# A hybrid attention and state-space block on one core: a recorded program with a list scheduler of its own, weight rings in 512-column blocks, and a tenth 7-product step in four gate pairs

## The chip, the core and the metric

The kernel runs on one NeuronCore of a Trainium2 chip; the other seven are idle. The metric is the device time of one execution in microseconds. Everything is float32 at the interface. PE is the matrix engine, DVE the vector engine, ACT the scalar engine, POOL the GpSimd engine (here it mostly starts transfers), SP the engine that starts most transfers.

## The reference, cut to what matters

One layer, 256 tokens, model width 4096:

```
h = rms_norm(x, pre_gain);  proj = h @ w_in          # 4096 x 24704
q, k, v, gate_a, qi, ki, wi, z, xs, bm, cm, dt, merge_logits = split(proj)
y_a = dsa_attention(rope(q), rope(k), v, rope(qi), rope(ki), wi) * silu(gate_a)   # top-64 keys by an indexer
y_b = ssd_mixer(xs, z, bm, cm, dt, ...)                                           # Mamba-2, chunked
g = sigmoid(merge_logits)                             # two gates of 4096 columns
out = (g[0] * (y_a @ w_branch_attn) + g[1] * (y_b @ w_branch_ssd)) @ w_out
x = x + rms_norm(out, post_gain)
```

Nearly all the work is in the products of 256 rows with the weights: 24,704 columns of w_in, then two branch projections (2048 to 4096) and w_out (4096 to 4096).

## The kernel before

Weights are streamed from HBM once, as float32. TensorE multiplies them in its rounding type fp32r: each operand is split into a rounded high part and a low part, and a product is three matmuls, low x high, high x low, high x high (`product`, line 598). A weight tile `raw` is split by ACT (the high part `wh`, line 548) and DVE (`wl` = raw - wh, line 552; line 550 where a sign is turned).

Big projections go in pairs of 512-column blocks (`pair_gemm`). The activations stand as 16 slots of 256 rows of the contraction (two k-tiles) by 256 tokens (two halves); one step of a pair takes one slot with a 2 x 2 block of weights (two k-tiles by two column blocks, each 128 x 512). Three kinds of steps:

- R: eight products, 24 matmuls. The weight blocks are split as they are, two at a time.
- D: also eight products, with one difference of the activations as an operand.
- S: seven products by Winograd's scheme, 21 matmuls. It needs sums and differences of the weights: POOL adds one block onto another by an accumulating transfer (line 672), DVE makes t2 (line 677) and then t3 and t4 together (line 678), and seven blocks instead of four are split. It also needs sums of the activations, kept ready in `ext` tiles for those slots that are S.

The tuples at the top of the program name the S slots of each stage: SX, SA, SS for the projections of h, SG for the gate pairs 3 to 6 (nine of 16 slots), SY for the branches, SM for the output. `SG_ORDER` is the order of the slots there.

Around the pairs runs side work: rotary, top-k, attention, the state-space scan, and the forms of the next stage's activations. It is written as generators; `step(pace)` advances the first of them after each step of a pair. Its matmuls (transposes, logits, scan products; called auxiliary below) are in plain fp32 and stand in PE's order between weight matmuls.

What sets the order: up to gate pair 1 the framework's scheduler, by priorities; from there on (`written`) the order of DVE and ACT is that in which the program is written, with the next step's first split started early (`begin`). Buffers: `raw` tiles of two blocks, eight of them (a ninth in the `late` pool from gate pair 2 on); `wh` and `wl` tiles of two blocks, five each (six late). The single block t2 takes a whole two-block tile early, and later a tile of its own, `nh` and `nl`, with one buffer.

A pair ends with evacuations: `early` (lines 602 to 604: an ACT copy and two DVE additions from PSUM), `late` and `rest`. The last pair is `ending`, followed by the last norm and the residual (`root_mean`, `final`).

Of the kernel before, what the change touches and what calls it, by code (L numbers as in the profile page):

```python
# [11 lines left out]
F32 = mybir.dt.float32  # L12
# [3 lines left out]
ALU = mybir.AluOpType  # L16
# [9 lines left out]
SBUFS = 5  # L26
RBUFS = 8
# [31 lines left out]
def fused_block(tc, x, xT, w_qi, w_misc, w_q0, w_qk, w_vg, w_x, w_z, w_gate, w_br, w_out2,  # L59
                percol, rows, tabs, tris, pgain, out):  # L60
    nc = tc.nc
# [24 lines left out]


# [39 lines left out]
    def step(n=1):  # L127
        credit[0] += n
        n = int(credit[0])
        credit[0] -= n  # L130
        while n and aux:
            try:
                next(aux[0])
            except StopIteration:
                aux.popleft()
            n -= 1
# [25 lines left out]
    rings = {"raw": (rawp, RBUFS), "wh": (whp, SBUFS), "wl": (wlp, SBUFS)}  # L162
    more_of, made = {}, {}

    def widen(pool, **counts):
        more_of.update({tag: (pool, n) for tag, n in counts.items()})
        made.update(dict.fromkeys(counts, 0))

    def ring(tag, shape, dtype):
        pool, n = rings[tag]  # L170
        if tag in more_of:
            second, m = more_of[tag]
            if made[tag] % (n + m) >= n:
                pool = second
                made[tag] += 1
                return pool.tile(shape, dtype, tag=tag, bufs=m, name=tag)
            made[tag] += 1
        return pool.tile(shape, dtype, tag=tag, name=tag)

    def raw_tile():  # L180
        return ring("raw", [P, HK, NW], F32)
# [8 lines left out]
    def gemm(chunks, nk, act, evac, prep=None, plan=None, done=None, pace=1, spill=()):  # L190
# [4 lines left out]
        plan = plan or [(h, (0, 1)) for h in range(nk // HK)]  # L195
        at = {t: [n for n, (_, tt) in enumerate(plan) if t in tt] for t in range(2)}
        raws, parts = {}, {}
        for n, (half, toks) in enumerate(plan):
            c, hf = divmod(half, KC // HK)
            if half not in raws:  # L200
                raws[half] = raw_tile()
                if prep is not None:
                    if not hf:
                        xr = prep_x(c)
                    load_half(raws[half], chunks[c], hf, c == 0)
                else:
                    load_half(raws[half], chunks[c], hf)
            if half not in parts:
                if half in spill:
                    wh, wl = (rawp.tile([P, HK, NW], F32R, tag="raw", name="wx") for _ in range(2))  # L210
                else:
                    wh = whp.tile([P, HK, NW], F32R, tag="wh", name="wh")
                    wl = wlp.tile([P, HK, NW], F32R, tag="wl", name="wl")
                parts[half] = wh, wl
                if len(parts) > SBUFS + len(spill):
                    del parts[next(iter(parts))]
                rs = raws[half]
                if prep is not None:
                    for i in range(HK):
                        split_x(half * HK + i, xr[:, hf * HK + i, :])  # L220
                        A.activation(wh[:, i, :], rs[:, i, :], AF.Copy)
                        V.tensor_sub(wl[:, i, :], rs[:, i, :], wh[:, i, :].bitcast(F32))  # L222
                else:
                    A.activation(wh, rs, AF.Copy)  # L224
                    V.tensor_sub(wl, rs, wh.bitcast(F32))  # L225
            wh, wl = parts[half]
            for i in range(HK):
                ah, al = act(half * HK + i)
                for t in toks:
                    first = n == at[t][0] and i == 0  # L230
                    last = n == at[t][-1] and i == HK - 1
# [11 lines left out]
    def gemm_misc(evac):  # L243
# [4 lines left out]
        for c in range(KT // KC):  # L248
            raw = rawp.tile([P, KC, P], F32, tag="raw", name="rawm")
            nc.sync.dma_start(raw, w_misc[c])  # L250
            wh = whp.tile([P, KC, P], F32R, tag="wh", name="whm")
            wl = wlp.tile([P, KC, P], F32R, tag="wl", name="wlm")
            A.activation(wh, raw, AF.Copy)
            V.tensor_sub(wl, raw, wh.bitcast(F32))
# [14 lines left out]
    warm = whp.tile([P, NW], F32, tag="wh", name="warm")  # L269
# [221 lines left out]
    def ext_forms(i, a, seven):  # L491
        a11, a21, a12, a22 = (a[:, k, t * P:(t + 1) * P] for k in range(2) for t in range(2))
        if i in seven:
            V.scalar_tensor_tensor(a22, a22, -1.0, a21, ALU.mult, ALU.subtract)
            V.tensor_sub(a21, a21, a11)
            V.scalar_tensor_tensor(a11, a22, -1.0, a11, ALU.mult, ALU.subtract)
            V.tensor_sub(a12, a11, a12)
            return a.rearrange("p k (t c) -> p (k t) c", t=2), 4
# [1053 lines left out]
```

## Time and profile before

| what | value |
|---|---|
| median of 3 runs | 2787.32 us (2786.72 to 2788.2) |
| span of the profiled execution | 2787.8 us |
| PE busy, PE weight loads busy | 2767.6 us (99%), 2277.0 us (82%) |
| DVE, ACT, POOL busy | 2458.2 us (88%), 1692.4 us (61%), 384.6 us (14%) |
| mean DMA rate | 235 GB/s |

Busy times are sums of instructions of one execution; TensorE's are pipelined, and their ends are modelled, so the distance between the starts of two matmuls says more than their duration (0.39 us for 128 x 512). A group's row gives its count, its busy time and mean duration, and the idle time of its engine just before it with what ended that. A row on a stretch of time gives for each engine the busy time and the number of instructions in it; an instruction on its border counts in both.

### The profile page before, as it was taken

To read this page: it belongs to the slowest core of one execution; us is meant where nothing else is said; L and a number is where in the kernel's file an instruction comes from. 1 tells how busy PE (TensorE), PEld (TensorE's weight loads), DVE (VectorE), ACT (ScalarE), POOL (GpSimd) and SP (SyncE) were. 2 spreads that over 40 slices of the span, in tenths; PEclk is the share of its full clock that TensorE was granted. 3 is DMA by queue.
4 is the path that set the end of the run, shared out by engine and by line. 5 is a ranking of instruction groups with operands and counts; after the bars stand their busy time and mean duration, and the time that the engine had idled before them with its cause. 6 is when DMAs were issued, how large, how long until landed. Compare 5 with 4: busy or idle time off the path is not lost.

```text
span 2787.8 us, 36296 instructions
## 1 busy us (share of the span) xinstructions
PE 2767.6 (99%) x12470; PEld 2277.0 (82%) x12470; DVE 2458.2 (88%) x3064; ACT 1692.4 (61%) x2217; POOL 384.6 (14%) x515
## 2 busy tenths in 40 slices
PE   9999999999999999999999999999999999999998
PEld 7877888888888888888887888888888887888886
DVE  6668989999999988887888888999999999998997
ACT  7444565565655666886677655556666545555554
POOL 0101101212112110111011111111111211220000
PEclk9999999999999999999999999999999999999999
DMA  9545787878878876666666688887888778978786
GB/s 375 194 167 171 212 241 219 261 226 234 243 222 253 227 225 217 203 197 214 197 194 200 230 257 247 247 250 238 272 270 257 251 250 253 318 229 242 240 253 209
DMA packets 206552, 655.37 MB, mean 235 GB/s; under 512 B 26272, under 2 KB 27552, under 8 KB 206368
## 3 DMA queue, kind: packets, MB, share of 16 engines
q1 hardware_dynamic: 163408, 565.74, 60.6%
q0 software_dynamic: 42240, 86.01, 14.8%
q8 instruction: 97, 1.59, 0.2%
q10 hardware_dynamic: 720, 1.31, 0.1%
q14 instruction: 87, 0.71, 0.1%
HBM read 627.79 MB, written 25.17 MB: 234 GB/s over the span
## 4 chain that ended last, share of the span: by engine, by line
PE 90%; DVE 4%; issue 3%; ACT 1%; DMA 1%; POOL 0%; POOLq 0%; SPq 0%; ACTq 0%; DVEq 0%
PE p L598 79%; PE p L233 3%; PE p L234 3%; PE p L235 3%; DVE wl L552 2%; ACT wh L548 1%; DMA raw<-w_gate_d 0%; PE p L438 0%; PE p L1033 0%; DVE raw L678 0%; PE p L898 0%; PE p L865 0%; DVE wl L225 0%; DVE raw L677 0%; PE p L1022 0%
## 5 line engine op out<-in xcount | busy, mean ns | idle before, releaser
L598 PE MATMUL p<-wh,b 128*128 128x512 f32 x4860 | 1608.0, 392 | 1.8 <-ACT wh L548 1.8
L548 ACT ACTIVATE wh<-raw 128x1024 fp32r<-128x1024 f32 (+1 forms) x1228 | 1193.5, 1016 | 514.4 <-PE p L598 235.8
L552 DVE TENSOR_TENSOR wl<-raw,wh 128x1024 fp32r<-128x1024 f32 (+1 forms) x965 | 1096.9, 1164 | 155.7 <-ACT wh L548 154.6
L598 PEld LDWEIGHTS p<-wh,b 128*128 128x128 f32 x4860 | 911.8, 188 | 193.2 <-ACT wh L548 6.4
L598 PE MATMUL p<-wl,b 128*128 128x512 f32 x2430 | 946.4, 389 | 0.7 <-DVE wl L550 0.7
L598 PE MATMUL p<-wh,ext 128*128 128x512 f32 x1958 | 692.9, 390 | 0.8 <-ACT wh L548 0.8
L598 PEld LDWEIGHTS p<-wl,b 128*128 128x128 f32 x2430 | 456.5, 188 | 95.4 <-DVE wl L550 2.4
L598 PEld LDWEIGHTS p<-wh,ext 128*128 128x128 f32 x1958 | 367.4, 188 | 78.5 <-ACT wh L548 2.7
L598 PE MATMUL p<-wl,ext 128*128 128x512 f32 x979 | 382.8, 391 | 1.0 <-DVE wl L552 0.8
L550 DVE SCALAR_TENSOR_TENSOR wl<-raw,wh 128x1024 fp32r<-128x1024 f32 x263 | 320.8, 1220 | 28.7 <-ACT wh L548 27.8
L548 ACT ACTIVATE nh<-raw 128x512 fp32r<-128x512 f32 x99 | 62.7, 633 | 319.0 <-DVE raw L677 267.7
L678 DVE TENSOR_TENSOR raw<-raw 128x1024 f32<-128x1024 f32 x200 | 244.5, 1222 | 5.4
L598 PEld LDWEIGHTS p<-wl,ext 128*128 128x128 f32 x979 | 183.7, 188 | 44.2 <-DVE wl L552 5.5
L233 PE MATMUL p<-wh,b 128*128 128x512 f32 x384 | 151.2, 396 | 1.8 <-DVE b L306 1.8
L234 PE MATMUL p<-wl,b 128*128 128x512 f32 x384 | 149.9, 390 | 0.0
L235 PE MATMUL p<-wh,b 128*128 128x512 f32 x384 | 149.6, 390 | 0.0
L225 DVE TENSOR_TENSOR wl<-raw,wh 128x1024 fp32r<-128x1024 f32 x80 | 99.4, 1243 | 52.8 <-ACT wh L224 52.6
L677 DVE TENSOR_TENSOR raw<-raw 128x512 f32<-128x512 f32 x200 | 137.7, 688 | 4.8
L224 ACT ACTIVATE wh<-raw 128x1024 fp32r<-128x1024 f32 x80 | 84.5, 1059 | 90.1 <-PE p L235 78.5
L672 POOL DMA_DIRECT2D raw<-w_gate_d x59 | 51.4, 871 | 487.8 <-DMA raw<-w_gate_d 208.5
L233 PEld LDWEIGHTS p<-wh,b 128*128 128x128 f32 x384 | 71.9, 188 | 20.2 <-issue 2.7
L234 PEld LDWEIGHTS p<-wl,b 128*128 128x128 f32 x384 | 72.1, 188 | 15.3 <-DVE wl L222 1.0
(255 smaller groups left out, 1937.7 us busy)
## 6 DMA issues: line engine op xcount, KB each, us to landing
raw<-w_gate_d SPq DMA_DIRECT2D x256, 512.0 KB, 6.0
raw<-w_vg_d SPq DMA_DIRECT2D x128, 512.0 KB, 5.3
raw<-w_x_d SPq DMA_DIRECT2D x128, 512.0 KB, 4.9
raw<-w_br_d SPq DMA_DIRECT2D x128, 512.0 KB, 6.0
raw<-w_out_d SPq DMA_DIRECT2D x128, 512.0 KB, 5.6
raw<-w_qk_d SPq DMA_DIRECT2D x96, 512.0 KB, 5.4
raw<-w_z_d SPq DMA_DIRECT2D x64, 512.0 KB, 5.2
raw<-w_qi_d SPq DMA_DIRECT2D x62, 512.0 KB, 5.9
```

The costliest lines, as they stand in the source:

```text
L224: A.activation(wh, rs, AF.Copy)
L225: V.tensor_sub(wl, rs, wh.bitcast(F32))
L233: T.matmul(ps[t], al[:, tk], wh[:, i, :], start=first, stop=False)
L234: T.matmul(ps[t], ah[:, tk], wl[:, i, :], start=False, stop=False)
L235: T.matmul(ps[t], ah[:, tk], wh[:, i, :], start=False, stop=last)
L548: A.activation(h, src, AF.Copy, scale=float(sign))
L550: V.scalar_tensor_tensor(l, src, -1.0, fbit(h), ALU.mult, ALU.subtract)
L552: V.tensor_sub(l, src, fbit(h))
L598: T.matmul(ps[j], l, r, start=first and n == 0, stop=left[j] == 0 and n == 2)
L672: G.dma_start(ra[:, 0, :], chunk(i)[:, HK, :], accum_op=ALU.add)
L677: V.tensor_sub(ra[:, 1, :], ra[:, 0, :], ra[:, 1, :])
L678: V.tensor_sub(rb, rb, ra[:, 1:2, :].to_broadcast([P, 2, NW]))
```

## The change

1. **Recording and scheduling.** `Plan` stands in for the engine queues. It records every instruction with the regions it reads and writes, and at the end of the program its `run` issues all of them in one order for all engines, with the framework's scheduler switched off. `run` is a list scheduler: at each turn it takes the engine that can start first, and on it the instruction of lowest priority number (place in the program, side work 20 places ahead) among those that its cost table says are ready; DVE and ACT put weight work first while PE has little ready work. An instruction of PE that side work feeds is held back by another 1.2 us.
2. **Rings.** One tile `raw0` of 16 blocks, `wh0` and `wl0` of 10 blocks each, used in a circle with any number of blocks at a time; four more blocks of wh and wl (`wh1`, `wl1`) from gate pair 2 to the output stage. No ninth raw tile, no `nh` and `nl`. An S step splits three blocks in one instruction, then two, then two (five DVE instructions instead of six), with the products in the order 2, 3, 1, 5, 6, 7, 4.
3. **Signs.** The D and R blocks are no longer split with a turned sign; evacuations and activation forms have plain sums and differences instead of scaled ones.
4. **Gate pairs 3 to 6** have ten S steps and six R steps instead of nine and seven, in the order R S S R S S R ... One more `ext` tile is made for it.
5. At the very end, one output weight tile is split twice rather than kept split.

```
-SBUFS = 5
-RBUFS = 8
+RAWN = 16
+SPLN = 10
+LATEN = 4
-SG = (1, 3, 5, 6, 8, 9, 10, 12, 14)
-SG_ADDED = (6, 9)
-SG_ORDER = (0, 1, 2, 3, 5, 4, 6, 7, 8, 9, 11, 10, 13, 12, 14, 15)
+SG = (1, 3, 5, 6, 8, 9, 10, 12, 13, 14)
+SG_ADDED = (6, 9, 13)
+SG_ORDER = (0, 1, 3, 2, 5, 6, 4, 8, 9, 7, 10, 12, 11, 13, 14, 15)
...
+        while todo:
...
+            at, e = best
+            can = [o for o in open_[e] if o.ready <= at + (near if e in ("DVE", "ACT") else 0)]
+            short = e in self.SHORT and max(free["PE"], at) + backlog < at + self.SHORT[e]
+            op = min(can, key=lambda o: (short and not o.main, o.prio))
...
-                ra, rb = loaded(n)
-                G.dma_start(ra[:, 0, :], chunk(i)[:, HK, :], accum_op=ALU.add)
-                b11, b21 = split(rb, 2)
-                t1, b22 = split(ra, 2)
+                raw = loaded(n)
+                G.dma_start(raw[:, 0, :], chunk(i)[:, HK, :], accum_op=ALU.add)
+                b22, b11, b21 = split(raw[:, 1:4])
...
-                V.tensor_sub(ra[:, 1, :], ra[:, 0, :], ra[:, 1, :])
-                V.tensor_sub(rb, rb, ra[:, 1:2, :].to_broadcast([P, 2, NW]))
+                V.tensor_sub(raw[:, 1, :], raw[:, 0, :], raw[:, 1, :])
+                V.tensor_sub(raw[:, 2:4], raw[:, 2:4], raw[:, 1:2].to_broadcast([P, 2, NW]))
...
-                t2, = split(ra[:, 1:2, :], 1)
-                if written:
-                    begin(n + 1)
-                t3, t4 = split(rb, 2)
+                t1, t2 = split(raw[:, 0:2])
+                t3, t4 = split(raw[:, 2:4])
...
-                for j in (2, 5, 3, 1, 6, 7, 4):
+                for j in (2, 3, 1, 5, 6, 7, 4):
...
+    with real_tc.manual_schedule():
+        tc.run()
```

In all, PE has 11,676 weight matmuls of 128 x 512 instead of 11,688. DVE has 1,253 splits instead of 1,448, on 2,670 blocks instead of 2,656. All recorded instructions carry line 330, the line that issues them.

Three places show how the order moves. First DVE in a gate pair (`wl` the low parts, `nl` the single block t2's, `raw<-raw` lines 677 and 678), before, two S steps and the R step between them:

```order
L677 TENSOR_TENSOR raw<-raw 128x512
L678 TENSOR_TENSOR raw<-raw 128x1024
L552 TENSOR_TENSOR nl<-raw,nh 128x512
L552 TENSOR_TENSOR wl<-raw,wh 128x1024 x3
L677 TENSOR_TENSOR raw<-raw 128x512
L678 TENSOR_TENSOR raw<-raw 128x1024
L552 TENSOR_TENSOR nl<-raw,nh 128x512
L550 SCALAR_TENSOR_TENSOR wl<-raw,wh 128x1024
```

and now, from an S step over the next one with an R step's splits behind it:

```order
L330 TENSOR_TENSOR wl_109<-raw_107,wh_108 128x1536
L330 TENSOR_TENSOR raw_107<-raw_107 128x512
L330 TENSOR_TENSOR raw_107<-raw_107 128x1024
L330 TENSOR_TENSOR wl_109<-raw_107,wh_108 128x1024 x3
L330 TENSOR_TENSOR wl_11978<-raw_107,wh_11977 128x1024
L330 TENSOR_TENSOR wl_109<-raw_107,wh_108 128x1536
L330 TENSOR_TENSOR raw_107<-raw_107 128x512
L330 TENSOR_TENSOR raw_107<-raw_107 128x1024
```

The single-block split is gone, three blocks go in one instruction, and the split of the untouched blocks (128x1536) now stands ahead of the step's two subtractions.

PE in the attention of the second head group (`pc,pT` are the products of values with transposed probabilities), before:

```order
L598 MATMUL p_5055<-wh,ext 128x512
L598 MATMUL p_5005<-wh,b_90 128x512
L598 MATMUL p_5005<-wl,b_90 128x512
L598 MATMUL p_5005<-wh,b_90 128x512
L898 MATMUL p_5589<-pc,pT 128x128 x4
L598 MATMUL p_4984<-wh,b_91 128x512
```

and now:

```order
L330 MATMUL p_4264<-wh_108,b_89 128x512
L330 MATMUL p_4708<-pc,pT 128x128
L330 MATMUL p_4264<-wl_109,b_89 128x512
L330 MATMUL p_4708<-pc,pT 128x128
L330 MATMUL p_4264<-wh_108,b_89 128x512
L330 MATMUL p_4256<-wh_108,ext 128x512
L330 MATMUL p_4708<-pc,pT 128x128
L330 MATMUL p_4256<-wl_109,ext 128x512
L330 MATMUL p_4708<-pc,pT 128x128
```

Four auxiliary matmuls that stood together now stand one by one between weight matmuls.

SP at the start (`xr` chunks of x transposed, `raw` the first weights; `ct`, `rw`, `tab`, `tabi` tables that are used later), before:

```order
L294 DMA xr<-xT_d 128x1024
L188 DMA raw<-w_qi_d 128x1024 x2
L294 DMA xr<-xT_d 128x1024
L188 DMA raw<-w_qi_d 128x1024 x2
L294 DMA xr<-xT_d 128x1024
L296 DMA ct<-tris_d 128x384
L297 DMA rw<-rows_d 128x96
L298 DMA tab<-tabs_d 128x2x256
L299 DMA tabi<-tabs_d 128x2x128
```

and now:

```order
L330 DMA xr<-xT_d 128x1024
L330 DMA raw_107<-w_qi_d 128x1024 x2
L330 DMA ct<-tris_d 128x384
L330 DMA rw<-rows_d 128x96
L330 DMA tab<-tabs_d 128x2x256
L330 DMA tabi<-tabs_d 128x2x128
L330 DMA xr<-xT_d 128x1024
L330 DMA raw_107<-w_qi_d 128x1024 x2
```

The four tables are now issued ahead of the third chunk of x instead of behind the fourth.

At the end of the program DVE's order has two of the products with the residual (line 1391 before) between the last evacuation from PSUM and the last norm, instead of one. On SP and POOL the number of transfers is the same but for four more accumulating ones.

More of the change, by code (lines that the diff above doesn't have):

```diff
@@ L1 @@
 from collections import deque
-from contextlib import ExitStack
+from contextlib import ExitStack, contextmanager
 import numpy as np
@@ L161, in fused_block, with halves, split @@
     live = deque()
[L162 to L181, printed above, removed]
+    def halves(src):
+        n = src.shape[1]
+        h, l = highs(n), lows(n)
+        A.activation(h, src, AF.Copy)
+        V.tensor_sub(l, src, fbit(h))
+        return h, l
+    def split(src):
+        h, l = halves(src)
+        return [(h[:, j, :], l[:, j, :]) for j in range(src.shape[1])]
     def load_half(raw, chunk, hf, each=False):
@@ L194, in gemm @@
         ps = {t: bank(accs[0][t]) for t in range(2)}
[L195 to L198, printed above, removed]
+        for half in range(nk // HK):
             c, hf = divmod(half, KC // HK)
[L200 to L226, printed above, removed]
@@ new lines, in gemm @@
+            raw = raws(HK)
+            if prep is not None:
+                if not hf:
+                    xr = prep_x(c)
+                load_half(raw, chunks[c], hf, c == 0)
+                wh, wl = highs(HK), lows(HK)
+                for i in range(HK):
+                    split_x(half * HK + i, xr[:, hf * HK + i, :])
+                    A.activation(wh[:, i, :], raw[:, i, :], AF.Copy)
+                    V.tensor_sub(wl[:, i, :], raw[:, i, :], fbit(wh[:, i, :]))
+            else:
+                load_half(raw, chunks[c], hf)
+                wh, wl = halves(raw)
@@ L227, in gemm @@
             for i in range(HK):
                 ah, al = act(half * HK + i)
-                for t in toks:
-                    first = n == at[t][0] and i == 0
-                    last = n == at[t][-1] and i == HK - 1
+                first = half == 0 and i == 0
+                last = half == nk // HK - 1 and i == HK - 1
+                for t in range(2):
                     tk = slice(t * P, (t + 1) * P)
@@ L248, in gemm_misc @@
         for c in range(KT // KC):
[L249 to L254, printed above, removed]
+            raw = raws(1)
+            nc.sync.dma_start(raw[:, 0, :], w_misc[c].rearrange("p k c -> p (k c)"))
+            wh, wl = (v.rearrange("p o (k c) -> p (o k) c", k=KC) for v in halves(raw))
             for i in range(KC):
@@ L645, in pair_gemm @@
         ended = []
[L646 removed]
         def loaded(n):
[L649 to L657 removed]
+            raw = raws(4)
+            for hf in range(2):
+                load_half(raw[:, 2 * hf:2 * hf + 2], chunk(plan[n][0]), hf)
+            return raw
         def first_of(n):
```

468 lines of the change are left out of this document (380 added, 88 removed).

## The prediction

> **What bounds the kernel now.** I read the page's busy shares first, then the stretches between two first evacuations of a pair of column blocks (line 602 marks them), then what TensorE's matmuls and weight loads waited for, then DVE's order of time inside one gate pair.
>
> ```profile
> PE 2767.6 (99%) x12470; PEld 2277.0 (82%) x12470; DVE 2458.2 (88%) x3064; ACT 1692.4 (61%) x2217; POOL 384.6 (14%) x515
> PEclk9999999999999999999999999999999999999999
> ```
>
> TensorE is never idle for long and its granted clock is full all through. A busy PE is not yet a PE at its peak, so the next view counts matmuls against time: the third of the four gate pairs that the change touches, then four halves of the branch projection.
>
> ```profile
> core 0: us, PE busy (x) PEld busy (x) DVE busy (x) ACT busy (x) POOL busy (x), PEclk, DMA share, GB/s
> 1857.00:1937.90 80.90, 80.90 (x359) 66.98 (x358) 75.07 (x77) 48.19 (x57) 9.98 (x13) 1.00 0.82 250
> ...
> 2184.50:2226.00 41.50, 41.50 (x185) 34.37 (x184) 40.91 (x48) 20.85 (x25) 13.05 (x19) 1.00 0.82 262
> 2226.00:2269.20 43.20, 42.40 (x184) 33.83 (x183) 40.16 (x45) 22.28 (x26) 3.44 (x4) 1.00 0.79 243
> ...
> 2311.30:2353.40 42.10, 41.35 (x179) 32.92 (x178) 40.43 (x45) 22.41 (x27) 3.42 (x4) 1.00 0.83 255
> ```
>
> The gate pair issues 9 x 21 + 7 x 24 = 357 weight matmuls in 80.9 us: 0.2266 us each, back to back, with DVE busy 75.07 us (93%). So there a matmul less is time less, as long as DVE keeps up. The row from 2226.0 has only 4 x 21 + 4 x 24 = 180 of them, worth 40.8 us, and takes 43.2: here PE waits, with DVE near full. The Trainium skill, "Perfetto Trace Analysis", section "Identifying the Most-Contended Engine", judges TensorE by the share of weight loading and not by matmul busy time; here that is 82%, and by it TensorE would have room and the 12 removed matmuls below would be worth 0 instead of 2.7 us. The gate row, with no gap between 357 matmuls, is what I go by.
>
> All waits of TensorE, as matmuls (first two rows) and weight loads (four largest groups) show them:
>
> ```profile
> PE p L598 <- ACT wh L548: 2.5, 7, 0.8
> PE p L598 <- DVE wl L552: 0.8, 1, 0.8
> ```
> ```profile
> L598 PEld LDWEIGHTS p<-wh,b 128*128 128x128 f32 x4860 | 911.8, 188 | 193.2 <-ACT wh L548 6.4 <-DVE pc L615 0.7
> L598 PEld LDWEIGHTS p<-wl,b 128*128 128x128 f32 x2430 | 456.5, 188 | 95.4 <-DVE wl L550 2.4
> L598 PEld LDWEIGHTS p<-wh,ext 128*128 128x128 f32 x1958 | 367.4, 188 | 78.5 <-ACT wh L548 2.7
> L598 PEld LDWEIGHTS p<-wl,ext 128*128 128x128 f32 x979 | 183.7, 188 | 44.2 <-DVE wl L552 5.5
> ```
>
> The loads waited 17.7 us in these groups, part of it behind a running matmul; the matmuls themselves only 3.3. Counting starts lies between: 73 intervals between neighbouring weight matmuls with no auxiliary one near are over 0.247 us (the first at 8.22, the last at 2732.26), together 13.7 us over 0.227. So about 13 us of waiting is all that a better order could win, under 0.5% of the span.
>
> ```profile
> 8.22 0.49 PE L234 MATMUL p<-wl,b 128*128 128x512 f32 x1
> ...
> 2732.26 0.50 PE L598 MATMUL p<-wl,ext 128*128 128x512 f32 x1
> ```
>
> **One S step more in four pairs.** It turns 24 matmuls into 21, four times: 12 x 0.2266 = -2.7 us. What it costs is DVE:
>
> ```profile
> 1804.13 4.62 DVE L552 TENSOR_TENSOR wl<-raw,wh 128x1024 fp32r<-128x1024 f32 x4
> 1808.79 0.69 DVE L677 TENSOR_TENSOR raw<-raw 128x512 f32<-128x512 f32 x1
> 1809.52 1.22 DVE L678 TENSOR_TENSOR raw<-raw 128x1024 f32<-128x1024 f32 x1
> 1810.66 0.68 DVE L552 TENSOR_TENSOR nl<-raw,nh 128x512 fp32r<-128x512 f32 x1
> 1811.26 1.22 DVE L550 SCALAR_TENSOR_TENSOR wl<-raw,wh 128x1024 fp32r<-128x1024 f32 x1
> ```
> ```profile
> DVE wl L552 <- ACT wh L548: 8.5, 15, 0.9
> DVE nl L552 <- ACT nh L548: 5.1, 6, 1.3
> DVE wl L550 <- ACT wh L548: 1.6, 6, 0.3
> ```
>
> Next starts give a two-block split 1.13 us ((4.62 - 1.22) / 3), one block 0.60, L677 0.73, L678 1.14. No row has a three-block split: between 1.13 (as two) and 1.13 + 0.60 = 1.73 (as two instructions); I take 1.13 + (1.22 - 0.68) = 1.67, a longer instruction. An S step was 3 x 1.13 + 0.60 + 0.73 + 1.14 = 5.86 and becomes 1.67 + 2 x 1.13 + 0.73 + 1.14 = 5.80; an R step stays 2.26. A pair goes from 9 x 5.86 + 7 x 2.26 = 68.6 to 10 x 5.80 + 6 x 2.26 = 71.6, so DVE's 75.07 becomes 78.1 while PE's 80.9 becomes 354 x 0.2266 = 80.2. DVE may idle 2.1 us a pair, where it idled 5.8. The waits above are of the three pairs from 1776.1 to 2018.8: 15.2 us, 5.1 a pair, 0.56 per S step. The 5.1 us of the single-block tile, whose one buffer goes, fall away. For the rest I follow an S step by the durations: L677 done at 0.69, ACT's two-block copy (1.05) at 1.8, while L678 ends at 1.9, so DVE waits about 0.1; and behind two S steps in a row the three-block copy (estimate: 1.05 + 0.4) is 0.3 late. Five S-S-R groups make 2.3 us: 80.4 against 80.2. Bounds: 0, and 0.56 x 10 = 5.6 us. I take the 2.3 and let PE lose 0.2 a pair, +0.8 in four.
>
> Changed at no cost: a subtraction in place of a scaled one (L550 and L552 both take 1.22 above); 195 fewer ACT splits, two more table loads and two more copies (ACT is busy 61%); four more accumulating DMAs (0.9 us each on POOL, busy 14%). Without these covers they would cost some 8 us. The raw ring falls from 18 blocks to 16. Its cover: the accumulation issued at 1796.34 is used by L677 at 1808.79, 12.4 us later, and lands in 6.6; half a step less (2.5 us) leaves 3.
>
> ```profile
> 1796.34 0.89 POOL L672 DMA_DIRECT2D raw<-w_gate_d  x1 [5.48 <-DVE raw L678]
> ```
> ```profile
> raw<-w_gate_d POOLq DMA_DIRECT2D x59, 256.0 KB, 6.6
> ```
>
> **Auxiliary matmuls split up.** The order now has 235 groups of plain fp32 matmuls between weight matmuls where it had 135.
>
> ```profile
> 113.73 0.39 PE L235 MATMUL p<-wh,b 128*128 128x512 f32 x1
> 113.96 0.27 PE L357 MATMUL p<-ct,mi 128*128 128x128 f32 x1
> 113.98 0.47 PE L233 MATMUL p<-wh,b 128*128 128x512 f32 x1
> 114.30 0.39 PE L234 MATMUL p<-wl,b 128*128 128x512 f32 x1
> ```
> ```profile
> 447.59 0.60 PE L887 MATMUL p<-ct,lm 128*128 128x128 f32 x4
> 447.94 0.47 PE L598 MATMUL p<-wh,b 128*128 128x512 f32 x1
> 448.26 0.39 PE L598 MATMUL p<-wl,b 128*128 128x512 f32 x1
> ```
>
> A lone transpose delays the stream by 114.30 - 113.96 - 0.227 = 0.11 us; four together by 448.26 - 447.59 - 0.227 = 0.44, the same 0.11 each. So a split costs nearly nothing; the bounds are 0 and 0.09 (the matmul behind a group starts its successor 0.32 after itself instead of 0.23). Nearest to the pair of rows I take 0.025, 2.5 us for 100. The index-score matmuls run in pairs that share the array, 16 in 1.09 us (143.40 - 142.31); some twelve lose the partner, 0.9 us.
>
> ```profile
> 142.31 1.16 PE L438 MATMUL p<-kiT,qiT 64*128 64x128 f32 x16
> 143.40 0.50 PE L233 MATMUL p<-wh,b 128*128 128x512 f32 x1
> ```
>
> **Both ends.** At the start four tables (0.64 MB by their shapes) move on SP from behind the fourth chunk of x to ahead of the third:
>
> ```profile
> 9.18 0.33 SPq L294 DMA_DIRECT2D xr<-xT_d  x1
> ...
> 13.54 0.43 SPq L296 DMA_DIRECT2D ct<-tris_d  x1
> ```
> ```profile
> 10.00:15.00 5.00, 3.94 (x17) 2.63 (x16) 3.74 (x9) 3.92 (x9) 0.00 (x0) 1.00 1.00 372
> ```
>
> SP itself waits for a free buffer until 9.18, so the issues are hidden; the DMA engines are full at 372 GB/s, so the third chunk is up to 1.7 us (0.64 MB / 372) later. Between 0 (PE then still has the second chunk) and 1.7, I take 0.5. At the end two products with the residual, not one, now stand between the last evacuation and the last norm:
>
> ```profile
> 2775.94 0.68 DVE L1437 TENSOR_TENSOR o<-o,p 128x512 f32<-128x512 f32 x1
> 2776.54 0.75 DVE L1391 SCALAR_TENSOR_TENSOR o<-o,oro,xr 128x512 f32<-128x512 f32 x1
> ...
> 2777.47 0.21 DVE L1374 TENSOR_SCALAR ov<-s,pre 128x1 f32<-128x1 f32 x1 [0.19 <-ACT osq L1372]
> ```
>
> One more is 0.6 to 0.75, less the 0.19 that DVE waited and a product that comes behind: +0.4.
>
> **PE's waits elsewhere.** A single recorded order for all engines, which may take any ready matmul, can remove waits that come from order but none that come from DVE's load. By order: the eight S-to-S joins of the attention pairs and the drained stretch before the third gate pair, some 7 of the 13 us; I let 5 go. By load: in the branch projection a half with four S steps keeps DVE busy 40 to 41 us of 41; one instruction less per S step is worth 0.06, so its 3.4 us fall by 1.4. Sum -6.4, bounds 0 and -13.
>
> Sum: -2.7 + 0.8 + 2.5 + 0.9 + 0.5 + 0.4 - 6.4 = -4.0. The profiled execution's span is 2787.8, 0.5 over the median of the runs (2787.32, of 2786.72 to 2788.2). 2787.8 - 4.0 = 2783.8 as a profile, 2783.3 as a median; as two of the small costs may well be 0, I say 2782.5.
>
> **Rivals.** *DVE bounds the gate pairs (slower).* If DVE idles 5.8 us a pair as now, a pair takes 78.1 + 5.8 = 83.9, 3.0 more than today, four times 12, in place of -1.9: 2782.5 + 13.9 = 2796.4. It decides from 2.1 us of idle a pair on; being in order, DVE holds all splits behind one late operand. For it: the 5.8 measured. Against it: DVE then was ahead of PE, and ACT's copies waited for PE. *The waits only move.* New order, same 13 us: 2782.5 + 6.4 = 2788.9, no change. For it: DVE at 98% of the branch halves, and still no three free blocks for an S step behind an S step. *All order waits go.* 13 us less the start's 1.7: another -5, 2777.5, or 2775.5 with no split cost. *Each DVE instruction costs its whole duration.* Then a pair's DVE is 10 x (1.76 + 2 x 1.22 + 0.69 + 1.22) + 12 x 1.22 + 8 x 0.68 = 81.2, 1.0 over PE, and +4.0 replaces -1.9: 2788.4. The Trainium skill, "VectorE: DVE Perf Modes", section "The DRAIN you can't avoid", says that the pipeline empties after every operation and that leaving out semaphores doesn't avoid it (with an exception for operations that no wait holds). Against it: four 1.22 us splits in 4.62.
>
> **Chances.** Forecast 0.42 (own range 2778 to 2787), order waits all gone 0.15, waits moved 0.21, whole durations 0.03, DVE bound 0.19. The bound of a measurement here is 0.2%, 5.6 us: faster is below 2781.7. Of the forecast 0.2 lies below, so faster 0.35; slower is the DVE rival with a little of the moved waits, 0.2; the rest, 0.45, same. The range leaves out a little at each end: 2775 to 2797.
>
> **What would show it.** 354 weight matmuls between first evacuations of the four pairs in 80.2 to 80.5 us with DVE busy about 78, waiting under 2.1; 81.5 or more means the DVE rival. Weight loads' waits for wh and wl half of today's or the same tells forecast from moved waits. A lone transpose should delay the stream by 0.13 us at most. The first continuous matmuls should come by 13.7 us. Wrong would be the forecast if transfers came late to raw (ACT or DVE waiting for DMA in the gates), which nothing here shows.

## The result: 0.6% slower, and the profile after

The changed kernel takes 2804.72 us (median of 4 runs, 2802.96 to 2806.66) against 2787.44 us of the kernel before (4 runs): a ratio of 1.0062, 95% interval 1.0049 to 1.0075. I had said 2782.5 us, 2775 to 2797. The profiled execution's span is 2803.3 us, 15.5 us over the 2787.8 of before. The medians differ by 17.3 us; what follows accounts for the 15.5 of the two profiled executions.

The page's busy shares of the changed kernel say nothing of it; TensorE is as busy as before and its clock as full:

```profile
PE 2780.6 (99%) x12458; PEld 2275.1 (81%) x12458; DVE 2458.4 (88%) x2883; ACT 1697.7 (61%) x2025; POOL 386.5 (14%) x519
...
PEclk9999999999999999999999999999999999999999
```

TensorE's lost time is read from the distances between the starts of its matmuls, as in the prediction: over a weight matmul's own 0.227 us, counted as *auxiliary* where an auxiliary matmul is near, and as *wait* where none is. By stage (the borders are counts of weight matmuls, the same in all kernels; a sum slightly below zero means a pitch of 0.2266), us. Some 11.6 us that all these kernels have alike, in the main the block of over a hundred auxiliary matmuls at 95 us, are left out:

| | start | index projections | attention pairs | z, x, first gates | ten-S gate pairs and the last | branches | output | all waits | auxiliary, index stage | auxiliary, rest |
|---|---|---|---|---|---|---|---|---|---|---|
| before | 1.7 | 0.2 | 4.2 | 3.4 | -0.7 | 3.2 | 1.1 | 13.1 | 20.0 | 71.5 |
| after | 1.0 | 0.2 | 10.5 | 1.1 | 3.3 | 0.5 | 3.3 | 19.8 | 28.6 | 72.3 |

With 0.9 us that the first weight matmul comes later, 1.1 behind the last one and 2.7 saved by 12 matmuls, the 15.5 us are 8.6 + 0.8 + 6.7 + 0.9 + 1.1 - 2.7 = 15.4.

**The 8.6 us: index scores cut up.** The changed kernel's time line of TensorE (start, duration; `x2` is two records):

```profile
138.59 0.48 PE L330 MATMUL p<-kiT,qiT 64*128 64x128 f32 x2
139.01 0.50 PE L330 MATMUL p<-wl,b 128*128 128x512 f32 x1
139.44 0.49 PE L330 MATMUL p<-kiT,qiT 64*128 64x128 f32 x2
139.85 0.72 PE L330 MATMUL p<-wh,b 128*128 128x512 f32 x2
140.51 0.49 PE L330 MATMUL p<-kiT,qiT 64*128 64x128 f32 x4
...
232.66 1.16 PE L330 MATMUL p<-kiT,qiT 64*128 64x128 f32 x16
233.75 0.50 PE L330 MATMUL p<-wh,b 128*128 128x512 f32 x1
```

In the block at 232.66, 16 records take 1.09 us, as before. Between weight matmuls, two records take 0.42 us (139.01 - 138.59), and the one weight matmul between two such groups takes 0.43 instead of 0.23. Three groups of 16 cost 3.33 us instead of 1.31 and two groups of 8 cost 2.51 instead of 1.28: 8.5 us, where I had priced them at 0.9. A group of 16 that is cut into five pays 2.02 / 4 = 0.5 us for each further piece, one of 8 that is cut into three 1.23 / 2 = 0.6.

**The waits.** Loads of weights wait longer for the low parts than before, and less for the high parts (total us, times, longest; first before, then now):

```profile
PEld p L598 <- ACT wh L548: 9.2, 20, 1.2
PEld p L598 <- DVE wl L552: 5.5, 12, 1.1
...
PEld p L598 <- DVE wl L550: 2.4, 7, 1.1
```
```profile
PEld p L330 <- DVE wl L330: 25.6, 57, 1.2
...
PEld p L330 <- ACT wh L330: 5.5, 17, 0.9
```

They stand at two kinds of places. One is the first S step of a pair in the attention part; here the last of them, DVE, then ACT, then PE:

```profile
826.85 0.69 DVE L330 TENSOR_TENSOR pc<-p,pc 128x512 f32<-128x512 f32 x1 [2.79 <-PE p L330]
...
828.59 3.07 DVE L330 TENSOR_TENSOR pc<-p,pc 128x512 f32<-128x512 f32 x5
...
831.91 1.75 DVE L330 TENSOR_TENSOR wl<-raw,wh 128x1536 fp32r<-128x1536 f32 x1
833.70 0.69 DVE L330 TENSOR_TENSOR raw<-raw 128x512 f32<-128x512 f32 x1
```
```profile
827.44 1.49 ACT L330 ACTIVATE wh<-raw 128x1536 fp32r<-128x1536 f32 x1 [3.99 <-PE p L330]
834.56 1.06 ACT L330 ACTIVATE wh<-raw 128x1024 fp32r<-128x1024 f32 x1 [5.62 <-DVE raw L330]
```
```profile
837.05 0.50 PE L330 MATMUL p<-wl,ext 128*128 128x512 f32 x1 [0.88 <-DVE wl L330]
```

DVE takes its instructions in the order of the program. It stands 2.79 us at an evacuation, then does five more of them and only then the S step's low parts and subtraction. ACT stood 3.99 us until PE had released three blocks of the ring, and then 5.62 until the subtraction was done. At 480.82 us the same evacuation stood for a store that had not landed:

```profile
480.82 0.69 DVE L330 TENSOR_TENSOR pc<-p,pc 128x512 f32<-128x512 f32 x1 [1.99 <-DMA yscr<-ysq]
...
483.76 1.75 DVE L330 TENSOR_TENSOR wl<-raw,wh 128x1536 fp32r<-128x1536 f32 x1
485.43 1.88 DVE L330 TENSOR_TENSOR pc<-p,pc 128x512 f32<-128x512 f32 x3
```

The other kind is an S step behind an S step, in the gate pairs and in the output stage. The four ten-S pairs (columns as in the prediction):

```profile
1708.00:1788.90 80.90, 80.90 (x357) 66.47 (x356) 76.65 (x70) 49.14 (x49) 10.78 (x14) 1.00 0.85 250
1788.90:1869.20 80.30, 80.30 (x354) 66.02 (x354) 77.05 (x71) 49.00 (x49) 10.84 (x14) 1.00 0.84 252
1869.20:1950.50 81.30, 81.06 (x357) 66.28 (x356) 77.17 (x71) 49.28 (x49) 10.80 (x14) 1.00 0.85 253
1950.50:2033.00 82.50, 81.55 (x356) 65.88 (x355) 77.93 (x71) 49.15 (x49) 10.82 (x14) 1.00 0.83 248
```

They take 325.0 us where four pairs of before took 4 x 80.9 = 323.6, with 12 matmuls fewer.

### The profile page after: what moved, and what is told of

Read it like the earlier page. It is cut to its first block, busy times and chain, and to the rows that moved or that the text cites. A ratio compares the mean times of both kernels' runs of the same rounds, so it can differ in the third digit from the quotient of the medians.

```text
span 2803.3 us, 35759 instructions
## 1 busy us (share of the span) xinstructions
PE 2780.6 (99%) x12458; PEld 2275.1 (81%) x12458; DVE 2458.4 (88%) x2883; ACT 1697.7 (61%) x2025; POOL 386.5 (14%) x519
## 3 DMA queue, kind: packets, MB, share of 16 engines
q10 hardware_dynamic: 720, 1.31, 0.1%
## 4 chain that ended last, share of the span: by engine, by line
PE 80%; DVE 9%; issue 5%; DMA 3%; ACT 2%; POOL 0%; POOLq 0%; DVEq 0%; SPq 0%; ACTq 0%
PE p L330 80%; DVE wl L330 5%; DVE raw L330 2%; DVE pc L330 1%; DMA raw<-w_br_d 1%; ACT wh L330 1%; DMA yscr<-ysq 1%; DMA raw<-w_out_d 1%; DMA raw<-w_gate_d 0%; DVE cacc L330 0%; ACT L330 0%; POOL yscr L330 0%; DVE hsq L330 0%; DMA hscr<-hsq 0%; DVE m L330 0%
## 5 line engine op out<-in xcount | busy, mean ns | idle before, releaser
L330 ACT ACTIVATE wh<-raw 128x1024 fp32r<-128x1024 f32 (+2 forms) x1253 | 1355.7, 1111 | 947.7 <-PE p L330 479.0
L330 PE MATMUL p<-wh,b 128*128 128x512 f32 x5596 | 1834.5, 391 | 1.2 <-DVE b L330 1.2
L330 DVE TENSOR_TENSOR wl<-raw,wh 128x1024 fp32r<-128x1024 f32 (+2 forms) x1253 | 1586.7, 1293 | 272.4 <-ACT wh L330 266.2
L330 PEld LDWEIGHTS p<-wh,b 128*128 128x128 f32 x5596 | 1050.1, 188 | 223.1 <-issue 3.3
L330 PE MATMUL p<-wl,b 128*128 128x512 f32 x2798 | 1094.3, 391 | 1.7 <-DVE wl L330 1.1
L330 PE MATMUL p<-wh,ext 128*128 128x512 f32 x2188 | 772.8, 393 | 0.6 <-ACT wh L330 0.5
L330 PEld LDWEIGHTS p<-wl,b 128*128 128x128 f32 x2798 | 525.5, 188 | 117.1 <-DVE wl L330 8.7
L330 PEld LDWEIGHTS p<-wh,ext 128*128 128x128 f32 x2188 | 410.0, 188 | 86.0 <-ACT wh L330 4.0
L330 PE MATMUL p<-wl,ext 128*128 128x512 f32 x1094 | 433.2, 397 | 4.0 <-DVE wl L330 3.5
L330 DVE TENSOR_TENSOR raw<-raw 128x512 f32<-128x512 f32 (+1 forms) x408 | 389.2, 954 | 10.0 <-DMA raw<-w_br_d 1.2
L330 PEld LDWEIGHTS p<-wl,ext 128*128 128x128 f32 x1094 | 205.4, 188 | 59.5 <-DVE wl L330 16.9
L330 DVE TENSOR_TENSOR pc<-p,pc 128x512 f32<-128x512 f32 x209 | 135.5, 682 | 9.9 <-DMA yscr<-ysq 5.9
L330 POOL DMA_DIRECT2D raw<-w_gate_d x63 | 55.0, 873 | 502.5 <-DMA raw<-w_gate_d 374.7
L330 POOL DMA_DIRECT2D raw<-w_x_d x22 | 19.1, 867 | 303.7 <-DMA raw<-w_x_d 303.7
L330 ACT ACTIVATE pc<-pc,rstd 128x512 f32<-128x512 f32 x72 | 48.1, 712 | 15.2 <-DVE pc L330 15.0
L330 POOL DMA_DIRECT2D raw<-w_vg_d x32 | 28.9, 902 | 205.7 <-DMA raw<-w_vg_d 136.9
L330 POOL DMA_DIRECT2D raw<-w_out_d x27 | 23.4, 868 | 237.5 <-DMA raw<-w_out_d 130.4
L330 POOL DMA_DIRECT2D hscr<-hsq x64 | 43.7, 720 | 88.3 <-DVE hsq L330 86.3
L330 POOL DMA_DIRECT2D mscr<-msq x64 | 42.8, 743 | 52.3 <-DVE msq L330 45.3
L330 ACT ACTIVATE ext<-fr 128x512 fp32r<-128x512 f32 (+1 forms) x39 | 21.7, 567 | 43.9 <-DVE fr L330 42.0
L330 POOL DMA_DIRECT2D yscr<-yb x64 | 37.6, 598 | 71.8 <-DVE yb L330 53.8
```

Of the source, the lines that this page charges most:

```text
L330: getattr(real, name)(*(fix(v) for v in args), **{k: fix(v) for k, v in kw.items()})
```

## Experiments

The runs are counted by their labels, e1 the first. All are edits of the changed kernel (added lines shift the line that issues everything from L330 to L342 in some); each was measured beside the kernel before on the same chip, which took 2787.5 to 2787.9 us there. The median of the changed kernel to set them against is 2804.7. Two runs that move the start alone are not in the table. The waits of the traces, by the stages of the table above:

| | time, us | start | attention | z, x, first gates | gate pairs | branches | output | all waits | auxiliary, index stage | auxiliary, rest |
|---|---|---|---|---|---|---|---|---|---|---|
| changed | 2804.72 | 1.0 | 10.5 | 1.1 | 3.3 | 0.5 | 3.3 | 19.8 | 28.6 | 72.3 |
| e1_scores | 2798.75 | 0.9 | 10.2 | 1.1 | 3.1 | 2.4 | 3.5 | 21.4 | 20.0 | 73.1 |
| e2_all | 2794.24 | 1.5 | 10.0 | 1.1 | 2.8 | 0.0 | 3.2 | 18.8 | 20.0 | 70.6 |
| e3_store | 2800.76 | 0.7 | 5.0 | 1.2 | 3.7 | 1.1 | 3.9 | 15.7 | 28.6 | 72.9 |
| e4_nine | 2810.55 | 1.0 | 12.0 | 1.1 | -0.1 | 4.1 | 3.9 | 22.3 | 28.6 | 72.9 |
| e5_both | 2788.79 | 0.9 | 3.3 | 1.1 | 3.3 | 1.7 | 3.9 | 14.4 | 20.0 | 70.6 |
| e6_two_one | 2793.38 | 0.8 | 0.2 | 0.8 | -0.7 | 12.6 | 2.3 | 16.2 | 20.0 | 72.4 |
| e7_land | 2797.50 | 0.7 | 3.3 | 1.1 | 1.6 | 9.1 | 4.1 | 20.0 | 20.0 | 70.6 |
| e9_pool | 2780.57 | 1.5 | 0.2 | 0.7 | -0.7 | -0.2 | 2.5 | 4.3 | 20.0 | 72.5 |
| e10_three | 2790.25 | 1.5 | 3.5 | 1.0 | 4.8 | 0.1 | 5.3 | 16.4 | 20.0 | 70.6 |
| e11_nine | 2784.44 | 1.3 | 0.2 | 0.7 | -0.7 | 0.7 | 4.0 | 6.3 | 20.0 | 72.5 |

**Scores together.** The cuts come from the priority numbers: side work stands 20 places ahead of its own place, so its instructions and weight matmuls with the same numbers alternate. Here a group's matmuls get numbers between two neighbours (`block`), and the first waits for all that the others need:

```
+        if eng == "PE" and self.block is not None:
+            at = self.block + (at - self.block) / 100 - 0.5
...
+                nc.block = len(nc.ops)
                 for i in range(per):
...
+                nc.close()
```

> The changed kernel with one thing undone: the eight (or four) index-score matmuls of a group stand together in PE's order again, as before the change. Theory A (the pairing is what the change lost): in the changed kernel's trace five of the twelve score groups are cut up by weight matmuls, three of them cost 3.33 us instead of 1.31 and two 2.51 instead of 1.28, together 8.5 us; put together, the time falls by 8.5, to 2796.2 us (+-1.5). Theory B (my prediction's price, 0.075 us for a lost partner, so the 17 us went elsewhere): 2803.8 us.

2798.75 us, 6.0 less, where theory A said 8.5 (+-1.5). The trace has the whole price: 28.6 us of the index stage become 20.0, those of before. 2 us of it are given back in the branches, where the moved order made new waits. So theory A holds in the index stage, though not for the whole; theory B falls.

**All auxiliary matmuls together.** The same with every step of side work (`nc.block = len(nc.ops)` in `step`).

> All auxiliary matmuls of one step of side work stand together (137 groups instead of 235), the scores among them. Theory A (only the scores, which share the array by half its rows, cost anything when cut up; lone full-width transposes cost nothing extra): the same as with the scores alone put together, 2796.2 us (+-1.5). Theory C (my prediction's term, 0.025 us for each of the other 82 splits): 2 us lower than that, 2794.2. Theory D (holding side work back until its whole group is ready makes something late): higher than 2797.5.

2794.24 us, 4.5 less than with the scores alone. In the trace 2.4 of that are waits in the branches that are gone again, and 2.5 are auxiliary, of which 1.7 lie behind the start, in the attention and scan stages: 0.021 us for each of the 82 splits taken away. Theory C's 0.025 us a split fits, A's "nothing" doesn't. That the time itself is C's 2794.2 is luck: it was reckoned from 2796.2 for the run above, which took 2798.75.

**POOL's transfers planned later.** One number of the planner. It holds for all transfers of POOL, stores and accumulations alike:

```
-                        late += self.LAND
+                        late += 2500 if e == "POOL" else self.LAND
```

> The planner takes a transfer that POOL starts to land 2 us later than it thought (2500 instead of 500 ns behind the modelled end), nothing else. Theory E (the waits at the start of the v/gate pairs come from DVE standing at an evacuation whose target is still being stored, 5.9 us of DVE's waits): PE's waits at 480, 653, 826 and 1000 us fall by 3 to 5 us in all, 2800 to 2802 us. Theory F (they come from the rings: ACT's three-block split waits until PE has released three blocks, 1.3 to 4.0 us each): no change, 2804.7 (+-1.2).

2800.76 us, 4.0 less; the attention pairs' waits fall from 10.5 to 5.0. DVE's evacuations still stand for a store, but for less, 3.4 us in all instead of 5.9; here the one that stood 1.99 us at 480.82:

```profile
481.25 2.09 DVE L330 TENSOR_TENSOR pc<-p,pc 128x512 f32<-128x512 f32 x3 [1.00 <-DMA yscr<-ysq]
```

Theory E holds for half of PE's waits there; the other half stays, and the next runs say what it is.

**Nine S steps.** `SG`, `SG_ADDED` and `SG_ORDER` as before the change.

> The changed kernel with nine instead of ten S steps in the four gate pairs, slots and order as before the change. 12 matmuls more are +2.7 us. Theory G (DVE near its limit makes the waits of these pairs, 3.8 us more than before): they go, and the time is 2804.7 + 2.7 - 3.8 = 2803.6. Theory H (the waits come from the planner's order and the rings, whatever the share of S steps): 2807.4.

2810.55 us, 5.8 more, above both theories. In the gate pairs the waits go, as G said: 3.3 us become -0.1. That DVE's load is their cause is not shown by it, since the order changed with the number of S steps; runs below have ten S steps, a busier DVE and no such waits. But 3.6 more come in the branches, 2.9 of them at 2105 us, where ACT stood 2.25 us at a transfer of y and DVE and PE stood behind ACT. A changed stage moved waits into a later one whose program is the same.

**Both edits (all together, stores later).**

> Auxiliary matmuls of one step together (as in the second run) and POOL's transfers planned 2 us later (as in the third). If the two act on different waits the gains add: 2804.7 - 10.5 - 4.0 = 2790.2 us (+-1.5). If the stalls that the second leaves are partly the same, 2791.5 or more.

2788.79 us: they add, with 1.4 us to spare, and the change is level with the kernel before (ratio 1.0006, 0.9997 to 1.0014).

**Three blocks split as two and one.** On top of both:

```
-                b22, b11, b21 = split(raw[:, 1:4])
+                b11, b21 = split(raw[:, 2:4])
+                b22, = split(raw[:, 1:2])
```

> As the run before it (both), but an S step splits its three untouched blocks again as two and one, so six DVE splits' instructions as before the change instead of five. Theory I (a split of three blocks at once needs three free blocks of the ring and 1.49 + 1.76 us before the first product, and so makes the waits where an S step follows an S step: 0.3 to 0.4 us each, ten of them in the output stage, 3.3 us more in the gate pairs): 4 us less than that run, about 2786. Theory J (DVE's load is what the gate pairs wait for, so an instruction more, 0.06 us each in 40 S steps, is lost): no change or 1 to 2 us more, 2790 to 2792.

2793.38 us, 4.6 more, and yet theory I is right where it speaks: attention 3.3 to 0.2, gate pairs 3.3 to -0.7, output 3.9 to 2.3, together 8.7 us gone. The branches lose 10.9, in two blocks of waits. At the first, POOL and then DVE:

```profile
2202.14 5.78 POOL L342 DMA_DIRECT2D mscr<-msq  x9 [2.26 <-DMA mscr<-msq]
2207.91 0.97 POOL L342 DMA_DIRECT2D raw<-w_br_d  x1
```
```profile
2217.27 0.69 DVE L342 TENSOR_TENSOR raw<-raw 128x512 f32<-128x512 f32 x1 [6.44 <-DMA raw<-w_br_d]
```

Nine stores of 0.64 us stand on POOL ahead of the accumulating transfer that DVE's subtraction needs; DVE stands 6.44 us. Behind both blocks the clock that TensorE is granted is down to half for a while, which is part of the 12.6 us (the last section has the rows).

**All transfers planned later.** On top of both, `LAND` 2000 instead of 500.

> As the run with both, but all other transfers (SP's weight loads above all) are also planned 1.5 us later (2000 instead of 500 ns). Theory K (remaining waits come from transfers that land later than planned, as the S step's accumulated block at 2105 us in the nine-S run, where ACT and DVE stood before it): 2 to 4 us less than that run. Theory L (what is left comes from the rings and from the order of DVE, which longer estimates don't touch): the same within 1 us.

2797.50 us, 8.7 more: both theories miss. The gate pairs gain 1.7, but the branches get two blocks of waits as in the run above, the first at another place (5.7 us at 2302 and 3.4 at 2390), with 12 stores `mscr` on POOL in the 9 us ahead of the accumulating transfer at 2294.

**Tables at the start put back.** On top of both, the four tables are ordered behind the fourth chunk.

> As the run with both, but the four tables at the start are issued behind the fourth chunk of x again. The prediction gave their place ahead of the third chunk 0.5 us. If they delay the third chunk's landing, PE's waits in the first 20 us (1.0 us in the changed kernel) fall by 0.3 to 1.0; if DMA has room there, nothing changes (within 0.3 us in the trace's first 20 us, and within the noise in the time).

2789.01 us against 2788.79: nothing that the time shows. The first weight matmul comes at 7.10 us against 7.09. The 0.5 us that PE waited from 12.4 us on in the run with both are not there, but the first matmuls start 0.427 us apart instead of 0.227 in this profile, so PE comes there later, and the trace doesn't settle it.

**POOL's accumulations first.** On top of the split in two and one:

```
-            op = min(can, key=lambda o: (short and not o.main, o.prio))
+            op = min(can, key=lambda o: ((short or e == "POOL") and not o.main, o.prio))
```

> As the run with the split in two and one, with one thing more: on POOL the planner takes an S step's accumulating transfer ahead of the stores of side work. Theory M (that run's 12.6 us of waits in the branch projection, two blocks of 6 us at 2216 and 2387, come from DVE standing 6.4 us at a subtraction whose accumulating transfer stood on POOL behind nine stores mscr): the two blocks go and the time is 2793.4 - 11 = 2782.4 us (+-1.5), under the kernel before. Theory N (the transfer comes late because its own base load does, with DMA full, so its place on POOL is no matter): 2791 to 2795.

2780.57 us (10 runs), 12.8 less than without it and a little more than theory M had said; against the kernel before 0.9976 (0.9967 to 0.9986), so this version beats both. The branches' 12.6 us of waits are gone. (The edit takes any transfer of POOL first that isn't side work.) POOL at the same place, the accumulation now between the stores:

```profile
2202.11 0.94 POOL L342 DMA_DIRECT2D raw<-w_br_d  x1 [1.57 <-DMA raw<-w_br_d]
2202.74 4.86 POOL L342 DMA_DIRECT2D mscr<-msq  x7
```

And the four ten-S pairs of this run take 320.9 us, with DVE busier than in the changed kernel:

```profile
1690.00:1770.40 80.40, 80.40 (x357) 66.56 (x356) 78.97 (x81) 51.15 (x59) 9.96 (x13) 1.00 0.85 250
1770.40:1850.70 80.30, 80.30 (x356) 66.50 (x355) 78.26 (x81) 51.01 (x59) 10.82 (x14) 1.00 0.86 260
1850.70:1931.30 80.60, 80.60 (x358) 66.73 (x357) 78.67 (x81) 49.83 (x59) 11.67 (x15) 1.00 0.86 252
1931.30:2010.90 79.60, 79.60 (x353) 65.92 (x352) 77.83 (x79) 49.52 (x58) 9.95 (x13) 1.00 0.86 257
```

**Three blocks at once, POOL's accumulations first.** The pair to the run above.

> The same with POOL's accumulating transfers first, but S steps split three blocks at once as in the changed kernel: against the run beside it the cost of the three-block split alone. Theory I (three blocks at once make the waits of S behind S): 6 to 8 us more than that run, 2788 to 2790, with 3.3 us of waits in the attention pairs, 3.3 in the gate pairs, 3.9 in the output stage where the other has about 0, -0.7 and 2.3. Theory J (the instruction saved is worth more): the same or less than that run.

2790.25 us: against the run beside it the three-block split costs 9.7 us, more than theory I's 6 to 8. Waits are 16.4 against 4.3, auxiliary 1.9 less. The four runs with and without each of the two edits say more than any pair of them: 2788.79 with neither, 2793.38 with the split in two and one, 2790.25 with POOL's accumulations first, 2780.57 with both. Each alone loses: two and one without the other has the branches' 12.6 us of waits, POOL's order without the other keeps the waits of the three-block split. So 9.7 and 12.8 us are what each is worth beside the other, and not by itself.

An S step behind an S step in the output stage shows how; first the changed kernel (ACT, DVE, PE's weight loads), then the run with two and one (ACT, DVE), whose PE comes to the same matmul at 2662.24 instead of 2684.3:

```profile
2681.15 1.49 ACT L330 ACTIVATE wh<-raw 128x1536 fp32r<-128x1536 f32 x1 [1.76 <-PE p L330]
...
2682.68 1.76 DVE L330 TENSOR_TENSOR wl<-raw,wh 128x1536 fp32r<-128x1536 f32 x1 [2.02 <-ACT wh L330]
...
2684.49 0.19 PEld L330 LDWEIGHTS p<-wl,b 128*128 128x128 f32 x1 [0.22 <-DVE wl L330]
...
2687.61 0.19 PEld L330 LDWEIGHTS p<-wl,b 128*128 128x128 f32 x1 [0.52 <-DVE wl L330]
```
```profile
2657.72 1.06 ACT L342 ACTIVATE wh<-raw 128x1024 fp32r<-128x1024 f32 x1 [0.94 <-PE p L342]
2659.76 0.63 ACT L342 ACTIVATE wh<-raw 128x512 fp32r<-128x512 f32 x1 [0.98 <-PE p L342]
...
2658.82 1.22 DVE L342 TENSOR_TENSOR wl<-raw,wh 128x1024 fp32r<-128x1024 f32 x1 [0.77 <-ACT wh L342]
```

Three blocks start 3.2 us ahead of PE, when the third of them is released, and take 1.49 + 1.76 us; two start 4.5 us ahead and are done in 2.3. The first product is hardly late by it (its load stood 0.22 us, beside a running matmul); PE loses most 3 us later, at the products of the next split, which DVE reaches late: the matmul behind the load at 2687.61 starts 0.48 us after the one before it.

The split in two and one has a cost of its own that the table counts as auxiliary (72.4 and 72.5 against 70.6). In each attention pair one group of eight auxiliary matmuls takes 0.7 us more, since its last two stand for an evacuation by DVE; here in the run with POOL's accumulations first:

```profile
460.11 0.49 PE L342 MATMUL p<-pc,pT 128*128 128x128 f32 x2 [0.45 <-DVE yat L342]
```

**Nine S steps, all else mended.**

> As the run with two and one and POOL's accumulations first, with nine S steps in the gate pairs. With the waits of the gate pairs gone, the tenth S step should be worth what TensorE's count says: 12 matmuls, 2.7 us. Expected by that 2.7 us more than the run with ten, about 2785. If DVE's load in ten-S pairs (78 of 80.3 us) costs something there, the difference is 1 us or less.

2784.44 us, 3.9 more: 2.7 by the matmuls, and waits of 6.3 us instead of 4.3, 1.5 of the difference in the output stage. The gate pairs have none with nine and none with ten. The tenth S step pays in full; DVE doesn't charge for it.

**ACT's order at the start.** On top of the run with POOL's accumulations first, ACT makes the first activation form ahead of the second high part.

> As the run with two and one and POOL's accumulations first; ACT at the start makes the first activation form ahead of the second weight's high part, as before the change. The first weight matmul came at 7.04 us instead of 6.11 because ACT stood 0.75 us at the second weight tile's landing. If that wait is the cause, the first matmul comes 0.7 to 0.9 us earlier and the whole 0.5 to 0.9 us shorter; if x's landing is, nothing changes.

2780.43 us (9 runs) against 2780.57: no difference that can be told, where 0.5 to 0.9 us were expected. The first matmul comes earlier, at 6.45 us (7.04 in the changed kernel). First the changed kernel (ACT, PE), then this run's PE:

```profile
5.24 0.63 ACT L330 ACTIVATE wh<-raw 128x512 fp32r<-128x512 f32 x1 [0.75 <-DMA raw<-w_qi_d]
...
7.04 0.50 PE L330 MATMUL p<-wh,b 128*128 128x512 f32 x1 [1.17 <-DVE b L330]
7.38 0.39 PE L330 MATMUL p<-wl,b 128*128 128x512 f32 x1
```
```profile
6.45 0.80 PE L342 MATMUL p<-wh,b 128*128 128x512 f32 x1 [0.58 <-DVE b L342]
7.04 0.63 PE L342 MATMUL p<-wl,b 128*128 128x512 f32 x1
7.47 1.06 PE L342 MATMUL p<-wh,b 128*128 128x512 f32 x2
```

But its second to eleventh matmuls start 0.43 us apart (7.47 - 7.04) instead of 0.23, and the run without the edit has eight matmuls at such a pitch. The start of the 145th weight matmul is at 41.30 us here, 42.12 in the run without the edit, 40.90 in the changed kernel and 40.83 before the change. So the 0.9 us of the changed kernel's first matmul are nearly gone by then; what ACT's order is worth stays open, under a microsecond.

## Why the prediction was wrong, point by point

| step | said, us | shown, us |
|---|---|---|
| 12 matmuls fewer | -2.7 | -2.7 |
| gate pairs' DVE | +0.8 | +4.0, and not by DVE's load |
| 100 splits of auxiliary matmuls | +2.5 | +1.7 for 82 of them; +0.8 with all that moved there |
| index scores | +0.9 | +8.6 |
| start | +0.5 | +0.9 later, 0.7 less waiting: +0.2 (+0.1 at the 145th matmul) |
| tail | +0.4 | +1.1 |
| other waits of PE | -6.4 | +3.5 (attention +6.3, z, x and first gates -2.3, branches -2.7, output +2.2) |

By this table the forecast (-4.0) and the profile (+15.5) are 19.5 us apart. Two terms make 17.6 of them, PE's waits elsewhere 9.9 and the index scores 7.7; the gate pairs make 3.2.

- **Index scores: mis-sized by 7.7 us.** I saw that scores would lose their neighbours in the order and priced a lost partner, 0.075 us. The price is on entering and leaving: 0.5 us a piece. Before's block could have told: its 16 records start in eight pairs 0.11 us apart, which is 0.9 of the 1.31 us that it costs; the other 0.4 are its ends. The Trainium skill, "TensorEngine Tiling (Array Packing)", section "Key Properties", says that changing the tiling mode drains TensorE; the first run agrees in that pieces cost and partners don't (20.0 us against 28.6). These matmuls use 64 rows of the array (`64*128` in the row), all others 128. That the rows are what counts is argued from this: full-width matmuls in plain fp32, cut up in the same way, cost 0.02 us a piece; no run changes the shape alone. The bound of this term had to be the number of pieces times 0.5 us, not the number of partners.
- **PE's waits elsewhere: the sign was wrong, and this is the largest miss, 9.9 us.** I argued that a recorded order can remove what order causes, and put bounds of 0 and -13 on it, so nothing above 0. In the changed kernel two things made new waits: a store planned to land too early (4.0 us by the third run, with evacuations on DVE standing for it) and the three-block split (attention pairs and output stage). The first is the planner's. Stores ahead of accumulations on POOL are the planner's too, but they cost nothing to speak of in the changed kernel itself (0.5 us of waits in the branches); they came with the edits. What I said could be won was there: with all three mended, waits fall from 13.1 to 4.3 us, by 8.8, between my 6.4 and the 11.3 of the rival "all order waits go"; 1.0 of it comes back as auxiliary. My working of the 6.4 was loose as well: the eight S-to-S joins hold 2.5 us in before's trace and the drained stretch at 1467 us 2.2, not "some 7".
- **The three-block split** I priced by DVE's throughput alone, 1.67 us instead of 1.13 + 0.60, and so as a gain. Its pitch is right (483.76 to 485.43 in the changed kernel's DVE is 1.67 us). Its cost is the time from three free blocks to the products, of this split and of the next ones behind it on DVE: 9.7 us by the tenth run against the ninth. "Still no three free blocks for an S step behind an S step" stood in my rival of moved waits, with no price.
- **The gate pairs.** DVE's busy time of about 78 us was right (76.65 to 77.93). The rival that DVE bounds them at 83.9 us is refuted: in the ninth run DVE is busy 77.83 to 78.97 us and the pairs take 79.6 to 80.6. Where I took 80.4, 320.9 / 4 = 80.2 came out there. The changed kernel's 81.25 take both the three-block split and the tenth S step in its order: with the split in two and one (sixth and ninth run) or with nine S steps (fourth run) the waits are gone.
- **Splits of full-width matmuls**: right in size, 0.021 us a split where I took 0.025.
- **Start.** The tables cost nothing that the time shows (the eighth run). The first matmul comes 0.9 us later, where ACT stands 0.75 us at the second weight tile ahead of the first activation form, which I hadn't looked at; little of it lasts.
- **Tail.** A product with the residual goes ahead of the last evacuation, and two more stand between it and the norm's first step on DVE:

```profile
2789.93 0.75 DVE L330 SCALAR_TENSOR_TENSOR og<-og,oro,xr 128x512 f32<-128x512 f32 x1
2790.60 0.68 DVE L330 TENSOR_TENSOR o<-p,o 128x512 f32<-128x512 f32 x1
2791.20 0.74 DVE L330 SCALAR_TENSOR_TENSOR og<-og,oro,xr 128x512 f32<-128x512 f32 x1
```

  The last norm is 0.54 us later after the last matmul than before; the rest of the 1.1 us is behind the last transfer's issue. The profiles of all runs with ten S steps and the three-block split have it (13.5 to 13.7 us from the last matmul to the end); those with two and one, or with nine S steps, don't (13.1). Why is not shown.
- **Moved waits**, 2788.9 us, was the nearest rival in kind, and its upper end was too low: it let waits move and not grow.

The ninth run against the kernel before, by the same count of the profiles (2779.4 and 2787.8 us): -2.7 for the matmuls, -8.8 for waits, +1.0 auxiliary, +1.6 at the start, +0.5 at the end, -8.4 in all. By the medians it is -6.9 us. That this mended kernel lands near the forecast's -4.0 doesn't confirm the sum: it has the three-block split undone, and the terms are others.

## What to carry to other kernels

When an order is made by a planner of your own, read its order for two things that its cost table doesn't know: matmuls of another array shape cut up between full ones, and transfers on one queue that an in-order engine will wait for behind transfers that nobody waits for. An instruction over more blocks saves an overhead and costs a longer wait for its inputs and for the first result: price both. Try two suspects together as well as one by one: here each mended alone lost time, and both together won 8.2 us. Put a bound above zero on every "this can only remove waits".

## What the runs showed of the hardware that I had not expected

- One piece of 64-row fp32 matmuls between 128-row ones costs 0.5 to 0.6 us beside its own work, and the weight matmul between two pieces takes 0.43 us; a lone full-width transpose costs 0.02 us more than one in a group.
- In eight of the fourteen profiles (the ninth, tenth and twelfth run among them; neither before nor the changed kernel) six to ten of the first dozen weight matmuls start 0.427 us apart instead of 0.227, up to 2 us in all. The granted clock goes with it. In three of them (second, ninth, tenth run) its record is at 0.50 for just this stretch; in the other five the record starts only at the stretch's end (10.1 to 10.9 us), and the column's 1.00 ahead of that is no reading. In the six others it is at full from 4.7 to 6.5 us on, ahead of the first weight matmul. Half the clock comes back in mid-run where PE stood for some microseconds: in the sixth run from 2218.0 to 2224.8 us and from 2392.1 to 2395.5, where eleven matmuls lose 0.2 us each, and in the seventh from 2307.1 to 2310.5. The ninth run's start, then the sixth run's first block, four matmuls in a microsecond where the changed kernel has six (columns as above):

```profile
9.00:10.00 1.00, 1.00 (x4) 0.79 (x3) 0.68 (x2) 0.63 (x1) 0.00 (x0) 0.50 0.86 283
```
```profile
2222.00:2223.00 1.00, 1.00 (x4) 0.80 (x3) 1.00 (x2) 1.00 (x3) 0.00 (x0) 0.50 0.66 193
```

  The Trainium skill, "TensorE: Matmul & The Clock Gate", section "What's actually happening", has the array at half rate until it has been busy for about 3.4 us; 0.427 us is what half rate makes of 512 columns by its figures, and the records at 0.50 among weight matmuls agree: they last 3.41 us, one of them 6.82. Why the record starts earlier in some executions than in others was not told apart.
